# Recurrent stage of a two-layer encoder: units in cycles of two tiles, weights rounded by a second load, no products on GpSimd

## The chip, the cores and the metric

One core of one Trainium2 chip. The metric is the device time of one execution in microseconds (us): the median of three executions. One more execution was profiled, and every row below comes from that one.

## What is computed

An encoder trunk of two layers over 512 tokens of width 1024, in float32. Layer 0 mixes tokens with a bidirectional gated linear recurrence, layer 1 with dilated window attention; a convolutional feed-forward block follows each. The change lies in the recurrent mixer alone:

```
gate, u = split(x @ w_in, 2)                       # 1024 -> 2 x 1280
u = depthwise_conv(u, conv_w, conv_b)              # width 4
# per direction d (forward, backward), per block of 80 channels
r = sigmoid(ub @ w_a[d] + b_a[d]);  i = sigmoid(ub @ w_x[d] + b_x[d])
log_a = -8 * softplus(-lam[d]) * r;  a = exp(log_a)
h_d = scan(h <- a*h + sqrt(-expm1(2*log_a)) * (i*u))   # backward: from the end
y = gelu(gate) * (h_fwd + h_bwd);  out = y @ w_out  # 1280 -> 1024
```

After it come `layer_norm(alpha*x + out)` and the feed-forward block.

## The kernel before

**Tiles.** The 1280 channels of the recurrence are ten tiles of 128 channels by 512 tokens. A matrix product is made of float32 operands that are each split into two parts of the matmul's format fp32r, `hi` (rounded) and `lo` (the rest), and three passes: hi·hi, hi·lo, lo·hi (`passes`, L203). A weight piece of 128x1024 takes three steps: a DMA into `wraw`, a rounding into `whi` (L149 on VectorE for odd pieces, L151 on ScalarE for the others), and the subtraction into `wlo` on VectorE (L152). `weights(i)` keeps pieces loaded six units ahead and split three ahead (`RGA`).

**Units.** TensorE works through thirty units, each 24 matmuls of 512 columns: `u` (ten units, the convolution's input), `g` (gates: four banks r, i, r, i of six matmuls, forward then backward) and `y` (the GeLU branch, banks named `gb`). `SEQ` sets their order; u0 and u1 are made ahead in halves by `first_units`. After them comes the product with `w_out` (`token_phase`: ten pieces; five of them over all tokens, then five more token tile by token tile, `RTAIL`).

**Work of one tile.** `conv(t)`: ScalarE scales the bank (L445), VectorE adds three taps (L448), ScalarE makes `hi` (L337), VectorE `lo` (L338). A gate unit reads the tile's own pair and the neighbour's channels; for tiles 1, 2, 3, 6, 7, 8 these are put together into `side` by two VectorE copies (L467, L468). `g_unit(t)`: sigmoids (L493) and tanh (L496) on ScalarE, then i·u on GpSimd (L501). `decay` takes groups of 2, 3, 3 and 2 tiles (`SUBS`): exp (L517) on ScalarE, its square on GpSimd (L519; on VectorE, L523, for the last two tiles), weight (L524) on VectorE, root (L529) on ScalarE, then for each tile i·u times the weight (L533), two scans (L535, L536) on VectorE and their sum on GpSimd (L537). The GeLU branch is copied out of its bank (L561), turned by GeLU (L567) late and multiplied (L577), then split (L580, L585).

**What sets the order.** Every engine runs its instructions in the order in which the program issues them, and waits at the head of its queue. In the stage this order is that of the loops, with `decay`'s steps put off by hand-written counts of ticks (`DL`, `SP`, `SPE`, `PSP`; a tick is three matmuls). Loads stand on SP's queue; a gate piece is first cleared by GpSimd (L192) and then filled by 6 to 10 small DMAs (L196). Buffers of 4 KB per partition come from an arena of 40 slots, and 8 PSUM banks from another.

Of the kernel before, what the change touches and what calls it, by code (L numbers as in the profile page):

```python
# [56 lines left out]
def encoder(ctx: ExitStack, tc: tile.TileContext, x, ln_g, ln_b, rg_w_in, rg_conv_w, rg_conv_b,  # L57
# [73 lines left out]
    raws, parts, dead = {}, {}, set()  # L131
    at = {"load": 0, "split": 0}

    def load_to(i):
        while at["load"] <= min(i, len(loaders) - 1):
            j = at["load"]
            raws[j] = sb.get([128, 1024], F32, "wraw")
            loaders[j](raws[j])
            at["load"] += 1

    def split_to(i, pool=False):
        while at["split"] <= min(i, len(loaders) - 1):
# [3 lines left out]
            hi = sb.get([128, 1024], F32R, "whi")  # L146
# [5 lines left out]
            (nc.gpsimd if pool else nc.vector).tensor_tensor(lo, raw, f(hi), OP.subtract)  # L152
            sb.put(raw)
# [54 lines left out]

    queues = []
# [80 lines left out]
    def token_phase(i0, lhs, nk, free_lhs, last=False, tail=TAIL):  # L290
# [3 lines left out]
        def mm(t, h, k):  # L294
            if k == 0:
# [3 lines left out]
                   [v[:, 512 * h:512 * h + 512] for v in w], k == 0, k == nk - 1)  # L299

# [88 lines left out]
    SUBS = (1, 4, 7, 9)  # L389
    SEQ = "u0 u1 u2 g0 u3 u4 u5 g1 u6 y0 g2 u7 g3 g4 u8 g5 u9 g6 y1 g7 y2 g8 y3 g9 y4 y5 y6 y7 y8 y9"  # L390
    SEQ = [(u[0], int(u[1])) for u in SEQ.split()]
    DL = (4, 6, 3, 4, 1)
    SP = 4
    SPE = 2
    PSP = 1
# [3 lines left out]
    def add_rglru():  # L399
        for kind, t in SEQ:  # L400
            if kind == "g":
                add_gates(t)
            else:
                add_cols(rg_w_in[0], (DR if kind == "u" else 0) + 128 * t)
# [3 lines left out]
    def rglru(i0, raw, load_next):  # L408
# [70 lines left out]
        def g_unit(t):  # L479
            sd, own = side(t)  # L480
# [5 lines left out]
            for m in range(4):  # L486
# [6 lines left out]
                nc.scalar.activation(dst[:, d], b, AF.Sigmoid, bias=tab[:, bias + d * NR + t:bias + d * NR + t + 1])  # L493
                ps.put(b)
                if m % 2 == 0:
                    nc.scalar.activation(th[t][:, d], r[t][:, d], AF.Tanh, scale=p8[:, d * NR + t:d * NR + t + 1])  # L496
            done(i)
            if own:
                sb.put(sd)
            u = u32[t][:, t % 2]  # L500
            nc.gpsimd.tensor_tensor(ii[t], ii[t], u[:, None, :].to_broadcast([128, 2, 512]), OP.mult)  # L501
            if t % 2:
                sb.put(u32[t])
# [5 lines left out]
        def decay(sub):  # L509
            e2 = {}  # L510
            n = len(sub)
            end = sub[-1] == NR - 1
            for t in sub:
                e2[t] = sb.get([128, 2, 512], F32, "e2")
                for d in range(2):
# [605 lines left out]
```

## Time and profile before

| | us |
|---|---|
| median of 3 executions | 1602.05 |
| lowest, highest | 1598.27, 1602.62 |
| the profiled execution | 1604.17 |
| its span in the trace | 1602.40 |
| TensorE busy, share of the span | 1554.2, 97% |
| VectorE, ScalarE, GpSimd busy | 957.6, 646.5, 198.9 |
| mean granted TensorE clock | 0.992 |

A busy engine in such a page is one that had an instruction under way. TensorE's mean says little about one stage: the recurrent stage is the first 217 us, and has to be read in stretches of its own. Brackets behind a row of a timeline give the idle time of that engine just before the row, and what ended it.

### The profile page before, as it was taken

How to read it: one execution, taken by the hardware profiler on the slowest of the kernel's cores; microseconds unless marked ns; L12 is line 12 of the kernel's file. 1: busy time of each engine (PE TensorE's matmuls, PEld its weight loads, DVE VectorE, ACT ScalarE, POOL GpSimd, SP SyncE). 2: the span in 40 equal slices, each digit the busy share in tenths (PEclk: the TensorE clock that was granted, in tenths of full speed). 3: DMA queues.
4: the chain of work that ended last, by engine and by line, in shares of the span. 5: the costliest groups of instructions: out<-in, count | busy, mean ns of one | idle time of the engine just before them, and what ended most of it. 6: DMA issues, size and time to landing. Idle time of an engine off the chain costs nothing.

```text
span 1602.4 us, 20933 instructions
## 1 busy us (share of the span) xinstructions
PE 1554.2 (97%) x8115; PEld 1317.3 (82%) x8115; DVE 957.6 (60%) x1323; ACT 646.5 (40%) x1051; POOL 198.9 (12%) x379
## 2 busy tenths in 40 slices
PE   7987889999999999999999999999999999999998
PEld 6866668988888888989889988988988888888886
DVE  5689985554444324567567578567667444445225
ACT  3567651333333321355365355455452333334210
POOL 2254411100000001103001001201202000000001
PEclk9999999999999999999999999999999999999999
DMA  4222273222223331324343524333524322223311
GB/s 139 70 53 69 74 234 92 80 80 79 80 78 108 128 118 48 98 80 150 100 119 102 148 80 128 124 104 94 169 86 146 88 79 79 79 79 111 134 71 53
DMA packets 211151, 161.49 MB, mean 101 GB/s; under 512 B 16846, under 2 KB 189164, under 8 KB 211052
## 3 DMA queue, kind: packets, MB, share of 16 engines
q1 hardware_dynamic: 209900, 155.96, 32.0%
q0 software_dynamic: 1152, 4.19, 0.8%
q8 instruction: 64, 1.05, 0.3%
q14 instruction: 35, 0.29, 0.1%
HBM read 137.05 MB, written 2.10 MB: 87 GB/s over the span
## 4 chain that ended last, share of the span: by engine, by line
PE 82%; DVE 8%; ACT 3%; issue 3%; POOL 2%; DMA 1%; SPq 1%; DVEq 0%; ACTq 0%; POOLq 0%
PE v L205 22%; PE o L205 20%; PE g L205 15%; PE qk L205 15%; DVE wlo L152 2%; PE tP L878 2%; PE oT L906 1%; PE oT L903 1%; DVE th L536 1%; PE s L773 1%; PE u L205 1%; PE s L772 1%; PE q L205 1%; DVE th L533 1%; PE k L205 1%
## 5 line engine op out<-in xcount | busy, mean ns | idle before, releaser
L152 DVE TENSOR_TENSOR wlo<-wraw,whi 128x1024 fp32r<-128x1024 f32 x247 | 314.4, 1283 | 200.4 <-ACT whi L151 167.5
L151 ACT ACTIVATE whi<-wraw 128x1024 fp32r<-128x1024 f32 x237 | 246.2, 1052 | 115.8 <-PE o L205 105.7
L205 PE MATMUL o<-whi,h 128*128 128x512 f32 x704 | 217.3, 389 | 0.0
L205 PEld LDWEIGHTS o<-whi,h 128*128 128x128 f32 x704 | 132.1, 188 | 27.5
L205 PE MATMUL qk<-xhi,whi 128*128 128x512 f32 x352 | 146.1, 415 | 0.0
L205 PE MATMUL g<-xlo,whi 128*128 128x512 f32 (+1 forms) x384 | 144.6, 376 | 1.5 <-DVE xlo L280 1.5
L205 PE MATMUL g<-xhi,whi 128*128 128x512 f32 (+1 forms) x384 | 144.5, 376 | 0.3 <-ACT xhi L279 0.2
L205 PE MATMUL v<-xhi,whi 128*128 128x512 f32 (+1 forms) x384 | 144.5, 376 | 0.0
L205 PE MATMUL v<-xhi,wlo 128*128 128x512 f32 (+1 forms) x384 | 144.3, 376 | 0.0
L205 PE MATMUL g<-xhi,wlo 128*128 128x512 f32 (+1 forms) x384 | 144.3, 376 | 0.0
L205 PE MATMUL v<-xlo,whi 128*128 128x512 f32 (+1 forms) x384 | 144.3, 376 | 0.0
L205 PE MATMUL qk<-xhi,wlo 128*128 128x512 f32 x352 | 139.4, 396 | 0.0
L205 PE MATMUL qk<-xlo,whi 128*128 128x512 f32 x352 | 139.0, 395 | 0.0
L205 PE MATMUL o<-wlo,h 128*128 128x512 f32 x352 | 136.9, 389 | 0.0
L349 DVE SCALAR_TENSOR_TENSOR t<-g,fft,t 128x511 f32<-128x511 f32 x44 | 33.0, 750 | 116.7 <-ACT t L347 116.6
L205 PE MATMUL v<-whi,xhi 128*128 128x256 f32 x352 | 100.8, 286 | 0.0
L205 PE MATMUL v<-whi,xlo 128*128 128x256 f32 x352 | 99.2, 282 | 0.0
L205 PE MATMUL v<-wlo,xhi 128*128 128x256 f32 x352 | 99.1, 281 | 0.0
L803 ACT ACTIVATE P<-P,stats 128x256 f32<-128x256 f32 x128 | 63.6, 498 | 80.8 <-DVE stats L801 80.7
L347 ACT ACTIVATE t<-g,fft 128x512 f32<-128x512 f32 x44 | 34.2, 778 | 138.0 <-PE g L205 138.0
L205 PEld LDWEIGHTS g<-xlo,whi 128*128 128x128 f32 x384 | 72.2, 188 | 16.2 <-DVE xlo L280 1.9
L205 PEld LDWEIGHTS g<-xhi,whi 128*128 128x128 f32 x384 | 72.2, 188 | 14.9 <-ACT xhi L279 0.8
(205 smaller groups left out, 3150.5 us busy)
## 6 DMA issues: line engine op xcount, KB each, us to landing
wraw<-in_ff_w_up_dram SPq DMA_DIRECT2D x88, 512.0 KB, 3.7
wraw<-in_at_w_qkv_dram SPq DMA_DIRECT2D x72, 512.0 KB, 4.3
wraw<-in_ff_w_down_dram SPq DMA_DIRECT2D x44, 512.0 KB, 3.2
wraw<-in_rg_w_in_dram SPq DMA_DIRECT2D x20, 512.0 KB, 4.7
V<-vst SPq DMA_DIRECT2D x128, 64.0 KB, 2.1
k<-k SPq DMA_DIRECT2D x48, 128.0 KB, 2.2
kl<-kl SPq DMA_DIRECT2D x48, 128.0 KB, 2.2
wraw<-in_rg_w_out_dram SPq DMA_DIRECT2D x10, 512.0 KB, 3.3
```

Of the source, the lines that this page charges most:

```text
L151: nc.scalar.activation(hi, raw, AF.Copy)
L152: (nc.gpsimd if pool else nc.vector).tensor_tensor(lo, raw, f(hi), OP.subtract)
L205: nc.tensor.matmul(o, lhs[a], rhs[b], start=start and n == 0, stop=stop and n == 2, skip_group_check=skip)
L347: nc.scalar.activation(t1, bg, AF.Identity, bias=tab[:, 3 * NF + fi:3 * NF + fi + 1], scale=tab[:, NF + fi:NF + fi + 1])
L349: nc.vector.scalar_tensor_tensor(t1[:, 1:], bg[:, :511], tab[:, fi:fi + 1], t1[:, 1:], op0=OP.mult, op1=OP.add)
L533: nc.vector.tensor_tensor(h, h, ii[t], OP.mult)
L536: nc.vector.tensor_tensor_scan(h[:, 1, ::-1], r[t][:, 1, ::-1], h[:, 1, ::-1], 0.0, OP.mult, OP.add)
L772: nc.tensor.matmul(b[:, c], qa[:, h, c], ka[:, h, c], start=True, stop=False)
L773: nc.tensor.matmul(b[:, c], qa[:, h, c], kl[:, h, c], start=False, stop=True)
L803: nc.scalar.activation(P[:, b, :], P[:, b, :], AF.Exp, bias=st[:, w, 0, h, b:b + 1], scale=0.125, accum_out=st[:, w, 1, h, b:b + 1])
L878: nc.tensor.transpose(tb[:, 128 * n:128 * n + 128], a, ident)
L903: nc.tensor.matmul(ov0, v(0, s), pt[:, n, 0:256].rearrange("p (b r i) -> p r b i", b=2, r=4), start=(s == 0 and n == 0), stop=False, skip_ ...
```

## The change

1. **Order of units.** `SEQ` becomes cycles of two tiles: two `u`, two `g`, two `y`. The input units run one cycle ahead.
2. **Rounded weights.** For `u` and `y` pieces from the seventh on (16 pieces) a second DMA, issued by GpSimd, loads the same 512 KB of DRAM into the fp32r tile `whi` (`rounded`); the rounding on VectorE or ScalarE goes. Other pieces are all rounded by ScalarE.
3. **No products on GpSimd.** i·u and the sum of the two scans go to VectorE, the square of the exponential goes to ScalarE. GpSimd keeps clearing gate pieces, the small preparation of the decay rates, and the new loads.
4. **Neighbours' channels** (`side`) are put together by two SP DMAs in place of two VectorE copies.
5. **GeLU** is read straight from the bank, for two tiles at a time; the decay chain runs for pairs.
6. **Pieces.** The side work is cut into single pieces with a rank, a cost and what they depend on. `pump`, called at every tick, issues a piece on VectorE or ScalarE when that engine is booked less than 1.4 us ahead of the tick's planned time. `need` issues what a gate unit or the output product reads.

```diff
 def load_to(i):
             raws[j] = sb.get([128, 1024], F32, "wraw")
             loaders[j](raws[j])
+            if j in rounded:
+                his[j] = sb.get([128, 1024], F32R, "whi")
+                rounded[j](his[j])
 def split_to(i, pool=False):
+            hi = his.pop(j, None)
+            if hi is None:
+                hi = sb.get([128, 1024], F32R, "whi")
+                nc.scalar.activation(hi, raw, AF.Copy)
+                book("s", 1.05)
-            if j % 2 and j < 3 * NR:
-                nc.vector.tensor_copy(hi, raw)
-            else:
-                nc.scalar.activation(hi, raw, AF.Copy)
+    def take(eng, limit):
+        for p in sorted(side_work[eng]):
+            rank, n, cost, makes, deps, fn = p
+            if all(d in due and due[d] <= limit for d in deps):
+                side_work[eng].remove(p)
+                due[makes] = book(eng, cost, deps)
+                fn()
+                return True
+        return False
+    def pump():
+        now = clock[0] * TICK
+        for eng in ("s", "v"):
+            while side_work[eng] and booked[eng] <= now + SLK and take(eng, now + SLK):
+                pass
-    SEQ = "u0 u1 u2 g0 u3 u4 u5 g1 u6 y0 g2 u7 g3 g4 u8 g5 u9 g6 y1 g7 y2 g8 y3 g9 y4 y5 y6 y7 y8 y9"
+    SEQ = "u0 u1 u2 u3 g0 g1 y0 y1 u4 u5 g2 g3 y2 y3 u6 u7 g4 g5 y4 y5 u8 u9 g6 g7 y6 y7 g8 g9 y8 y9"
 def make_side(t):
-                nc.vector.tensor_copy(v[0:64], f(uhl[t + 1][0:64]))
-                nc.vector.tensor_copy(v[64:128], f(uhl[t - 1][64:128]))
+                nc.sync.dma_start(f(v[0:64]), f(uhl[t + 1][0:64]))
+                nc.sync.dma_start(f(v[64:128]), f(uhl[t - 1][64:128]))
 def g_unit(t):
+            need(("ul", max(t - 1, 0)), ("ul", t), ("ul", min(t + 1, NR - 1)))
-            nc.gpsimd.tensor_tensor(ii[t], ii[t], u[:, None, :].to_broadcast([128, 2, 512]), OP.mult)
+            def gated():
+                nc.vector.tensor_tensor(ii[t], ii[t], u32[t][:, t % 2][:, None, :].to_broadcast([128, 2, 512]), OP.mult)
 def decay(...)
-                    nc.gpsimd.tensor_tensor(e2[t], r[t], r[t], OP.mult)
+                nc.scalar.activation(e2[t], r[t], AF.Square)
-                nc.gpsimd.tensor_tensor(h[:, 0], h[:, 0], h[:, 1], OP.add)
+            def both(t):
+                nc.vector.tensor_tensor(th[t][:, 0], th[t][:, 0], th[t][:, 1], OP.add)
+            piece("s", 1, 4.1, ("a", pr), (("g", pr[-1]),), exps)
+            for t in pr:
+                piece("s", 1, 1.05, ("q", t), (("a", pr),), lambda t=t: square(t))
+                piece("v", 1, 1.22, ("w", t), (("q", t),), lambda t=t: weight(t))
+            piece("s", 1, 3.4, ("s", pr), tuple(("w", t) for t in pr), root)
 def y_unit(t):
-            nc.scalar.activation(ga[t][:, t % 2], b, AF.Gelu_apprx_tanh if direct else AF.Copy)
+                def gelu():
+                    for n in pr:
+                        nc.scalar.activation(ga[:, n % 2], yb[n], AF.Gelu_apprx_tanh)
+                        ps.put(yb.pop(n))
```

**Where it moves instructions.** VectorE at the start of the stage, before: behind the rates' `RECIPROCAL` stand tile 0 (taps, `lo`), tile 1 and then weights.

```order
L425 RECIPROCAL sp_s2_285<-sp_s2_285 128x20
L448 SCALAR_TENSOR_TENSOR u32_320<-u_137,rgt_281,u32_320 128x510
L448 SCALAR_TENSOR_TENSOR u32_320<-u_137,rgt_281,u32_320 128x511 x2
L338 TENSOR_TENSOR u_325<-u32_320,u_325 128x512
L448 SCALAR_TENSOR_TENSOR u32_320<-u_138,rgt_281,u32_320 128x510
L448 SCALAR_TENSOR_TENSOR u32_320<-u_138,rgt_281,u32_320 128x511 x2
L338 TENSOR_TENSOR u_332<-u32_320,u_332 128x512
```

The same place after the change; `wlo_394` belongs to y0's piece, the first that GpSimd loads, and L507 is the `lo` of tiles 0 and 1.

```order
L469 RECIPROCAL sp_s2_295<-sp_s2_295 128x20
L156 TENSOR_TENSOR wlo_340<-wraw_141,whi_338 128x1024
L156 TENSOR_TENSOR wlo_344<-wraw_191,whi_342 128x1024
L498 SCALAR_TENSOR_TENSOR u32_330<-u_131,rgt_291,u32_330 128x510
L498 SCALAR_TENSOR_TENSOR u32_330<-u_131,rgt_291,u32_330 128x511 x2
L498 SCALAR_TENSOR_TENSOR u32_330<-u_132,rgt_291,u32_330 128x510
L498 SCALAR_TENSOR_TENSOR u32_330<-u_132,rgt_291,u32_330 128x511 x2
L156 TENSOR_TENSOR wlo_394<-wraw_346,whi_348 128x1024
L507 TENSOR_TENSOR u_381<-u32_330,u_381 128x512
L507 TENSOR_TENSOR u_403<-u32_330,u_403 128x512
```

Three weights now stand ahead of the `lo` of tile 0, and the third reads a tile that GpSimd's DMA fills. GpSimd at that place, before: the last step of the rates (L436), the clearing of g1's piece, then products and clearings.

```order
L436 TENSOR_SCALAR sp_n8_286<-sp_p8_287 128x20
L192 MEMSET wraw_352 128x1024
L501 TENSOR_TENSOR i_408<-i_408,u32_320 128x1024
L192 MEMSET wraw_450 128x1024
L192 MEMSET wraw_541 128x1024
L192 MEMSET wraw_588 128x1024
L501 TENSOR_TENSOR i_597<-i_597,u32_320 128x1024
```

And after; the first clearing is that of g2's piece.

```order
L480 TENSOR_SCALAR sp_n8_296<-sp_p8_297 128x20
L176 DMA whi_348<-in_rg_w_in_dram 128x8x128
L176 DMA whi_352<-in_rg_w_in_dram 128x8x128
L176 DMA whi_356<-in_rg_w_in_dram 128x8x128
L176 DMA whi_398<-in_rg_w_in_dram 128x8x128
L202 MEMSET wraw_436 128x1024
L202 MEMSET wraw_499 128x1024
```

Four loads stand between the rates and g2's clearing. SP's queue after the change, at the end of g2's copies: `side_458` is tile 1's, `side_490` tile 2's.

```order
L206 DMA wraw_436<-in_rg_w_a_dram 16x2x64
L206 DMA wraw_436<-in_rg_w_x_dram 16x2x64
L527 DMA side_458<-u_432 64x1024
L528 DMA side_458<-u_381 64x1024
L527 DMA side_490<-u_481 64x1024
L528 DMA side_490<-u_403 64x1024
```

The neighbours' copies are new on this queue, and tile 1's stands behind g2's eight copies, which wait for the clearing.

## Rows read from the trace of the kernel before

**Rows 1.** Stretches: span, busy us (x instructions) by engine, clock, DMA share, GB/s.
```profile
26.19:217.01 190.82, 165.37 (x676) 128.56 (x674) 166.96 (x151) 116.97 (x159) 83.96 (x64) 0.96 0.25 70
40.39:51.59 11.20, 11.20 (x50) 9.01 (x49) 7.36 (x8) 7.40 (x10) 3.29 (x2) 1.00 0.43 110
57.18:62.64 5.46, 5.46 (x26) 4.50 (x24) 4.57 (x7) 1.30 (x2) 0.00 (x0) 1.00 0.50 125
141.80:146.97 5.17, 5.17 (x12) 4.08 (x13) 4.39 (x5) 5.10 (x8) 0.00 (x0) 0.51 0.40 99
```
**Rows 2.** Timeline of TensorE: start, us, instruction [idle before, what ended it].
```profile
141.80 1.19 PE L205 MATMUL gate<-u,whi 128*128 128x512 f32 x2 [6.95 <-DVE u L448]
217.01 0.49 PE L205 MATMUL o<-whi,y 128*128 128x512 f32 x1 [1.12 <-ACT whi L151]
```
**Rows 3.** Groups of TensorE, 26 to 240 us: busy us, mean ns | idle before.
```profile
L205 PE MATMUL gate<-u,whi 128*128 128x512 f32 x112 | 36.7, 408 | 14.3 <-DVE u L448 10.0 <-ACT u L337 2.2 <-ACT r L493 1.4
L205 PE MATMUL gate<-u,wlo 128*128 128x512 f32 x56 | 22.6, 404 | 1.3 <-DVE wlo L152 1.3
```
**Rows 4.** Groups of VectorE, 26.19 to 217.01 us.
```profile
L152 DVE TENSOR_TENSOR wlo<-wraw,whi 128x1024 fp32r<-128x1024 f32 x27 | 47.4, 1760 | 3.6 <-ACT whi L151 2.6
L524 DVE SCALAR_TENSOR_TENSOR th<-e,th 128x1024 f32<-128x1024 f32 x10 | 17.1, 1724 | 7.1 <-POOL e L519 7.1
L535 DVE TENSOR_TENSOR_SCAN th<-r,th 128x512 f32<-128x512 f32 x10 | 16.2, 1624 | 0.3
L448 DVE SCALAR_TENSOR_TENSOR u<-u,rgt,u 128x511 f32<-128x511 f32 x20 | 15.0, 750 | 0.7
```
**Rows 5.** Groups of GpSimd and ScalarE, the same stretch.
```profile
L501 POOL TENSOR_TENSOR i<-i,u 128x1024 f32<-128x1024 f32 x10 | 28.7, 2871 | 51.0 <-ACT i L493 41.1 <-issue 9.9
L151 ACT ACTIVATE whi<-wraw 128x1024 fp32r<-128x1024 f32 x14 | 14.7, 1049 | 0.0
L517 ACT ACTIVATE r<-r,sp_n 128x512 f32<-128x512 f32 x20 | 12.7, 711 | 0.0
L529 ACT ACTIVATE th<-th 128x1024 f32<-128x1024 f32 x10 | 10.2, 1054 | 10.9 <-DVE th L524 10.8
L517 ACT ACT_TABLE_LOAD x4 | 5.1, 1283 | 0.1
```
**Rows 6.** Timelines of VectorE, then of GpSimd.
```profile
34.94 0.69 DVE L338 TENSOR_TENSOR u<-u,u 128x512 fp32r<-128x512 f32 x1 [0.76 <-ACT u L337]
104.87 1.23 DVE L152 TENSOR_TENSOR wlo<-wraw,whi 128x1024 fp32r<-128x1024 f32 x1
110.16 3.47 DVE L152 TENSOR_TENSOR wlo<-wraw,whi 128x1024 fp32r<-128x1024 f32 x1
...
110.15 2.40 POOL L501 TENSOR_TENSOR i<-i,u 128x1024 f32<-128x1024 f32 x1 [0.89 <-ACT i L493]
```
**Rows 7.** Timeline of GpSimd: first and last step of the rates, what follows.
```profile
28.08 0.23 POOL L426 TENSOR_TENSOR sp_q<-sp_q,sp_s 128x20 f32<-128x20 f32 x1 [26.10 <-ACT u L445]
37.94 1.18 POOL L436 TENSOR_SCALAR sp_n<-sp_p 128x20 f32<-128x20 f32 x1
39.06 0.95 POOL L192 MEMSET wraw<- 128x1024 f32 x1
```
**Rows 8.** DMAs of 512 KB issued by GpSimd: ns of issue, us to landing.
```profile
L246 POOL DMA_DIRECT2D lng<-in_ln_g_dram x4: 595/599/777, 207.5 to 1464.1; - x4
...
DMA to landing us min/median/max: 4.3/4.5/5.2
```
**Rows 9.** DMAs issued by SP: KB each, median us to landing; one gate copy.
```profile
wraw<-in_rg_w_in_dram SPq DMA_DIRECT2D x20, 512.0 KB, 4.7
wraw<-in_rg_w_out_dram SPq DMA_DIRECT2D x10, 512.0 KB, 3.3
k<-k SPq DMA_DIRECT2D x48, 128.0 KB, 2.2
...
41.35 0.43 SPq L196 DMA_DIRECT2D wraw<-in_rg_w_x_dram  x1
```

More of the change, by code (lines that the diff above doesn't have):

```diff
@@ L206, in passes, with book, piece, need @@
                              skip_group_check=skip)
+    TICK, SLK = 0.69, 1.4
+    booked = {"v": 0.0, "s": 0.0}
+    due = {}
+    side_work = {"v": [], "s": []}
+    def book(eng, cost, deps=()):
+        start = max([booked[eng], clock[0] * TICK] + [due[d] for d in deps])
+        booked[eng] = start + cost
+        return booked[eng]
+    def piece(eng, rank, cost, makes, deps, fn):
+        heapq.heappush(side_work[eng], (rank, next(order), cost, makes, deps, fn))
+    def take(eng, limit):
[12 more added lines that the diff above has]
+                pass
+    def need(*keys):
+        for key in keys:
+            while key not in due:
+                assert take("s", 1e9) | take("v", 1e9), key
     queues = []
@@ L403, in add_rglru @@
             else:
-                add_cols(rg_w_in[0], (DR if kind == "u" else 0) + 128 * t)
+                add_cols(rg_w_in[0], (DR if kind == "u" else 0) + 128 * t, len(loaders) >= 6)
         for k in range(NR):
@@ L521, in weight, with inputs @@
             def weight(t):
-                if end:
-                    nc.vector.tensor_tensor(e2[t], r[t], r[t], OP.mult)
                 nc.vector.scalar_tensor_tensor(th[t], e2[t], 1.0, th[t], op0=OP.add, op1=OP.mult)
-                sb.put(e2[t])
+                sb.put(e2.pop(t))
             def root():
-                for t in sub:
+                for t in pr:
                     nc.scalar.activation(th[t], th[t], AF.Sqrt)
-            def scan(t):
+            def inputs(t):
+                nc.vector.tensor_tensor(th[t], th[t], ii[t], OP.mult)
+                sb.put(ii.pop(t))
@@ L538, in scan @@
-                sb.put(r[t])
-            now = clock[0] + (DL[0] if end else DL[1])
-            for m, t in enumerate(sub):
-                at_tick(now + DL[2] * m, lambda t=t: weight(t))
-            now += DL[2] * (n - 1) + DL[3]
-            at_tick(now, root)
-            for m, t in enumerate(sub):
-                at_tick(now + DL[4] + (SPE if end else SP) * m, lambda t=t: scan(t))
-            if end:
-                at_tick(now + 1, gelu)
-                for m in range(sub[0]):
-                    at_tick(now + DL[4] + SPE * n + PSP * m, ready)
@@ L570, in ready @@
[L570 to L587 removed]
+                sb.put(r.pop(t))
@@ new lines, in rglru @@
+        yb = {}
+        def y_unit(t):
+            yb[t] = bank("gb")
+            cols_unit(yb[t], next(it))
+            if t % 2:
+                pr = (t - 1, t)
+                ga = sb.get([128, 2, 512], F32, "ga")
+                left[pr] = 2
+                def gelu():
+                    for n in pr:
+                        nc.scalar.activation(ga[:, n % 2], yb[n], AF.Gelu_apprx_tanh)
+                        ps.put(yb.pop(n))
+                piece("s", 1, 2.7, ("ga", pr), (), gelu)
+                for n in pr:
+                    product(n, pr, ga[:, n % 2], ga)
@@ new lines, in product, with times, high, low @@
+        def product(t, pr, g, ga):
+            def times():
+                nc.vector.tensor_tensor(g, g, th[t][:, 0], OP.mult)
+                sb.put(th.pop(t))
+            def high():
+                y[t] = pair("y")
+                nc.scalar.activation(y[t][:, 0], g, AF.Copy)
+            def low():
+                nc.vector.tensor_tensor(y[t][:, 1], g, f(y[t][:, 0]), OP.subtract)
+                left[pr] -= 1
+                if not left[pr]:
+                    sb.put(ga)
+            piece("v", 3, 0.69, ("p", t), (("ga", pr), ("h", t)), times)
+            piece("s", 3, 0.63, ("yh", t), (("p", t),), high)
+            piece("v", 3, 0.69, ("yl", t), (("yh", t),), low)
```

142 lines of the change are left out of this document (64 added, 78 removed).

## Prediction

> **What bounds the kernel now.** I read the busy times by stretch first. TensorE is busy nearly all the span, so the change can win only what TensorE loses in the recurrent stage. That stage is read from unit u2, at 26.19 us, to the first matmul of the output product, at 217.01 us: 190.82 us, of which TensorE is busy 165.37 [rows 1]. Twenty-eight units lie in it. Two `u` units back to back take 11.20 us, so a `u` or `y` unit takes 5.60, and a gate unit takes 5.46 at full clock [rows 1]. Unhindered, the 18 units of the first kind and ten gate units need 18 x 5.60 + 10 x 5.46 = 155.4 us. **The stage loses 35.4 us**: 25.4 idle, and 10.0 at a lower clock, as after the longest wait (6.95 us [rows 2]), when two gate banks took 5.17 us at a granted clock of 0.51, the level of 1.2 GHz [rows 1]; at full clock two banks of four are half of 5.46, so that cost 2.4 us.
>
> Next, who is waited for. The longest waits end with VectorE (taps, weights) [rows 2, 3], which is busy 167 of the 191 us [rows 1]. Its groups show why: the subtraction into `wlo` takes 1.23 us alone and 3.47 beside GpSimd's product of i and u [rows 6]; its mean is 1.76, that of the weight 1.72, that of the scan 1.62 [rows 4]. Against 1.23, these three groups lose 27 x 0.53 + 10 x 0.49 + 10 x 0.39 = 23 us. GpSimd's i·u, for its part, takes 2.87 us [rows 5]. So VectorE sets the stage's pace, and GpSimd sets VectorE's.
>
> **The change, part by part.**
>
> *Products off GpSimd.* VectorE gets ten i·u of 1.23 us and ten sums of half that width, 0.69 as the `lo` of the same width [rows 6]: +19.2 us. It loses some 13 roundings (0.69 us where nothing stretches them, the time of a `lo`) and 12 neighbour copies of as much: -17.3 us. The squares it also loses are 2 x 1.23 us. So the count is even, and the stretching of at least 23 us goes: 167 - 23 = 144 us at most, over units that need 155. ScalarE gets ten squares, as long as a root of 1.05 us [rows 5], and about seven table loads of 1.28 us, since each of five cycles goes through sigmoid, exp, root and GeLU; it loses some ten half-width steps of the GeLU branch, under 0.71 us each: 117 + 10.5 + 9.0 - 6 = 130 us of work. Both then lie under TensorE's 155.4, and **TensorE becomes the bound**. What remains is waits.
>
> *Start of the stage.* This is a new wait. VectorE's queue has `wlo_394` ahead of the `lo` of tiles 0 and 1, and it reads a tile that GpSimd loads. GpSimd issues that load only after the rates, which ran from 28.08 to 39.06 us [rows 7]. Some of those small steps were stretched by VectorE (the last took 1.18 us, the first 0.23); now two `wlo` fall on earlier steps, so I take 38.2. Queued behind it on VectorE: both `lo`, and all of tile 2 and 3; who waits is g0. A load issued by GpSimd lands 4.5 us after issue [rows 8]; it was of 4 KB rows. With SP, 512-byte rows (`rg_w_in`) land 4.7 us after issue and 4 KB rows (`rg_w_out`) 3.3: +1.4 [rows 9]. Unknown is the issue: 0.60 us for 128 rows, and now 1,024 pieces. Its bounds are 0.6, if the count is nothing, and eight times the 0.60 to 0.78 of the rows, 4.8 to 6.2; I take 1.2, nearer to the row that is the same instruction with the same bytes, which adds 0.6. So it lands at 38.2 + 4.5 + 1.4 + 0.6 = 44.7; `wlo` 1.23 and `lo` 0.69 make 46.6. TensorE has ended u3 at 26.2 + 11.2 = 37.4: **9.2 us lost**, plus 2.4 for the clock as after the 6.95 us wait. Before, the wait there was 2.2 [rows 3], part of the 35.4.
>
> The Trainium skill (DMA: Bandwidth & Descriptors, Anatomy of one DMA) fits a load by GpSimd as 2.0 us plus its bytes over 436 GB/s, 3.2 us here. By it the sum would be 1.3 us lower. The row of 4.5 us speaks against it, and I keep the row.
>
> *Neighbours by DMA.* Tiles 1, 3 and 7 are read soon after they are made. After the first landing VectorE does the two `lo` (to 47.3), three taps of 0.75, a `wlo` and a `lo`: 51.5. A copy is half of 512 KB: between 2.2 us (128 KB) and 3.3 (512 KB) [rows 9], with its issue landed by 54.3 to 55.5. g1 asks at 46.6 + 5.46 + 2.4 + 0.7 = 55.2. For g3 and g7 the cover is a unit u, a unit g and one half bank, 11.8 us, over taps, `hi`, `lo`, a scan or two ahead in the queue and the copy, some 10. I put 1.0 us for the three, with 0 and 6 as ends.
>
> *Other loads by GpSimd.* They are issued six units ahead and split three ahead: three units, 16.8 us, cover about 6.5. Cost nothing; without the cover each load's landing would stand in VectorE's queue. DMA engines were 25% busy [rows 1], and 16 loads of 512 KB in some 160 us add 52 GB/s to 70.
>
> *Small waits.* Gate banks waited 1.4 us for ScalarE and 1.3 for `wlo` [rows 3]: I keep 3 us.
>
> *The end.* The last pair's chain and the ten `w_out` pieces now stand beside the output product, which reads the last five tiles only after five pieces over all tokens. From the end of g9 that is two y units and five pieces, 7 x 5.60 = 39.2 us. VectorE has in it two weights, two i·u, two inputs, four scans and ten `wlo` (20 x 1.23), two sums and some eight products and `lo` (10 x 0.69): 31.5 us; ScalarE has four exps, two squares, two roots, ten `whi`, three tables, and GeLUs and `hi` of some eight half widths: 2.8 + 2.1 + 2.1 + 10.5 + 3.8 + 5.7 = 27 us. Both fit, but one waits for the other in turn (exps, weights, roots, scans, products); walked through in the order of the two queues, the last `wlo` ends only about a microsecond before TensorE asks. I count no loss, with 0 and 4 us as ends.
>
> **Sum.** Losses after: 9.2 + 2.4 + 1.0 + 3.0 = 15.6 us; before: 35.4. The output product starts 19.8 us earlier, at 197.2. The rest of the program is the same code. The profiled execution took 1604.17 us (a span of 1602.40 and 1.77 around it), so the sum is 1584.4 for it; it was 2.12 above the median, and against the median of 1602.05 the forecast is **1582**.
>
> **Rivals.**
>
> *Dear issue (1598).* If an issue takes 5.5 us, the middle of the far bound, the first load lands at 49.0 and g0 starts its second pass at 50.9: 13.5 + 2.4. GpSimd's queue then has four issues, to 60.2, before it clears g2's piece; SP's has g2's eight copies of 0.43 behind that, and tile 1's neighbours behind those: 61.2 + 3.5 + 3.3 = 68, where g1 asks at 59.5. That is 8.5 + 2.4 more: 31 us lost, 1598. For it: GpSimd makes the pieces one by one in no row shown; against it: nothing shows the issue growing. Up to 2 us each it stays near the forecast.
>
> *Issue over 6.4 us: slower.* The same chain with an issue P: the neighbours land at 38.2 + 4P + 1 + 3.5 + 3.3, and 26 units and the clock follow, so the output product starts near 191.4 + 4P. At P = 6.4 that is 217, no change; at 8 us 223.4, **1608**. The trap is that side data stand behind loads that are in no hurry. The far bound, 6.2, ends just below. The Trainium skill (SBUF — State Buffer, the box on "DVE blocks DMA" under SBUF: two separate sides) says such issues starve, 0.62 us becoming 3.1, beside VectorE copies that use both ports; by it each of the first four issues would cost 2.5 us more. No row here shows that, and the change takes the copies and roundings from VectorE in this stage; 0.78 us is the slowest issue [rows 8].
>
> *Queues in step (1594).* The order is fixed by planned costs, and a piece that is late holds everything behind it. From the last sigmoid of a pair ScalarE has three tables, four exps, two squares, two `whi`, two roots and two GeLUs (0.71 each at most): 3.8 + 2.8 + 2.1 + 2.1 + 2.1 + 1.4 = 14.4 us before the next `u` can be scaled, under 2 y and 1 u, 16.8. If waits for VectorE in between take 5 us, four cycles lose 2.6 to 3 each: 12 us.
>
> *Does not pay (1602).* All of these at once, VectorE's queue staying the bound through waits in its head in place of stretching.
>
> **How the numbers follow.** Forecast 0.57 (1571 to 1590), queues in step 0.15, dear issue 0.10, no gain 0.10, slower 0.08. The low end: a start that loses 7 us with its clock (the rates over at 37, the load landing in the 4.5 of the row) and nothing else, 28.4 us won, and 2.5 of the output product's own waits and clock: 1571. The high end is the dear issue, 1598. About 0.3%, 4.8 us, is what a measurement of this kernel can tell from no change. Faster by more: forecast, queues in step and half the dear issue's 0.10 (cheaper than 5.5 us), 0.77; within: the other half and no gain, 0.15; slower: 0.08.
>
> **What would show it.** VectorE's `wlo`, weights and scans at 1.2 us throughout; a TensorE wait near 37 us ended by a `lo` at about 46 to 47, followed by a few us at half clock; GpSimd's loads at about 1 us of issue; hardly a wait above 2 us afterwards; the output product's first matmul near 197. Wrong would be: issues of 4 us or more, a second long wait in g1 ended by a DMA, waits of 3 us in every cycle ended by ScalarE, or waits within the output product for y8 and y9.

## The result, and the profile after

The changed kernel took 1577.82 us (median of four executions, 1574.23 to 1578.61), the kernel before 1600.91 beside it: a ratio of 0.9853, 95% interval 0.9831 to 0.9874, some 23 us less. The profiled executions differ by 25.6 us (1578.61 against 1604.17; spans 1576.8 and 1602.40). The stretches of the changed kernel that answer to [rows 1] are the recurrent stage and the output product up to its transposes (columns: span, busy us by engine TensorE, weight load, VectorE, ScalarE, GpSimd, granted clock, DMA share, GB/s).

```profile
26.18:195.20 169.02, 159.32 (x676) 128.31 (x674) 124.17 (x139) 126.88 (x165) 30.77 (x52) 0.97 0.65 160
195.20:250.50 55.30, 55.30 (x249) 45.82 (x248) 43.31 (x53) 19.11 (x23) 4.53 (x3) 1.00 0.42 126
```

The output product of the kernel before, cut in the same way:

```profile
217.01:275.06 58.05, 57.29 (x248) 47.10 (x249) 37.74 (x48) 16.51 (x21) 5.06 (x4) 0.97 0.46 147
```

**Where the time went.** The stage is 21.80 us shorter, the output product 2.75, and the remaining 1.05 lies in the unchanged rest. Against the 155.4 us that the units need, the stage loses 13.6 us where it lost 35.4: 169.02 - 159.32 = 9.7 idle and 3.9 at half clock. The idle part is three waits; these are all of them (timeline of TensorE; in brackets the idle time before the row and what ended it). The waits of [rows 2, 3] that ended with taps, `wlo` and sigmoids are gone. The 3.9 us at half clock are the rest of the 13.6; 3.5 of them are read off behind the first two waits (1.9 and 1.7, see the section on the prediction).

```profile
44.41 0.80 PE L215 MATMUL gate<-u,whi 128*128 128x512 f32 x1 [6.55 <-DVE u L507]
...
54.34 0.90 PE L215 MATMUL gate<-side,whi 128*128 128x512 f32 x2 [2.17 <-DMA side<-u]
...
90.46 0.70 PE L215 MATMUL gate<-side,whi 128*128 128x512 f32 x2 [0.97 <-DMA side<-u]
```

The groups of VectorE and GpSimd, 26 to 210 us, answer to [rows 4, 5] (busy us, mean ns of one, idle time before): each VectorE operation is back at the 1.2 us that it takes undisturbed, and the product of i and u is one of them.

```profile
L156 DVE TENSOR_TENSOR wlo<-wraw,whi 128x1024 fp32r<-128x1024 f32 x32 | 38.9, 1220 | 34.1 <-ACT whi L153 25.1 <-DMA whi<-in_rg_w_in_dram 7.2 <-PE gate L215 1.8
L570 DVE TENSOR_TENSOR i<-i,u 128x1024 f32<-128x1024 f32 x10 | 12.2, 1220 | 5.0 <-ACT i L554 4.9
L593 DVE SCALAR_TENSOR_TENSOR th<-e,th 128x1024 f32<-128x1024 f32 x10 | 12.0, 1220 | 4.4 <-ACT e L590 4.4
L610 DVE TENSOR_TENSOR_SCAN th<-r,th 128x512 f32<-128x512 f32 x9 | 10.9, 1207 | 0.0
...
L176 POOL DMA_DIRECT2D whi<-in_rg_w_in_dram x16 | 14.4, 907 | 60.8 <-DVE wlo L156 16.0 <-PE u L215 14.7 <-DVE th L601 11.7
```

The start of the stage, which the prediction worked out step by step: GpSimd's last step of the rates and its first four loads, VectorE's `wlo` that reads the first of them with both `lo` behind it, and SP's second copy for tile 1's neighbours.

```profile
37.75 0.26 POOL L480 TENSOR_SCALAR sp_n<-sp_p 128x20 f32<-128x20 f32 x1
37.95 3.80 POOL L176 DMA_DIRECT2D whi<-in_rg_w_in_dram  x4
...
42.53 1.23 DVE L156 TENSOR_TENSOR wlo<-wraw,whi 128x1024 fp32r<-128x1024 f32 x1 [7.16 <-DMA whi<-in_rg_w_in_dram]
43.67 1.29 DVE L507 TENSOR_TENSOR u<-u,u 128x512 fp32r<-128x512 f32 x2
...
49.53 0.60 SPq L528 DMA_DIRECT2D side<-u  x1
```

### The profile page after: what moved, and what is told of

It reads as the page before. It is cut to its first block, busy times and chain, and to the rows that moved or that the text cites. A ratio compares the mean times of both kernels' runs of the same rounds, so it can differ in the third digit from the quotient of the medians.

```text
span 1576.8 us, 20972 instructions
## 1 busy us (share of the span) xinstructions
PE 1545.2 (98%) x8115; PEld 1316.6 (83%) x8115; DVE 920.5 (58%) x1314; ACT 662.4 (42%) x1062; POOL 145.8 (9%) x367
## 3 DMA queue, kind: packets, MB, share of 16 engines
q8 instruction: 64, 1.05, 0.3%
## 4 chain that ended last, share of the span: by engine, by line
PE 89%; DVE 4%; issue 2%; POOL 1%; DMA 1%; ACT 1%; SPq 1%; DVEq 0%; POOLq 0%; ACTq 0%
PE v L215 23%; PE o L215 20%; PE g L215 16%; PE qk L215 15%; PE gb L215 3%; PE gate L215 2%; PE u L215 2%; PE tP L943 2%; PE oT L971 1%; PE oT L968 1%; PE s L838 1%; PE s L837 1%; PE q L215 1%; PE k L215 1%; PE tx L323 1%
## 5 line engine op out<-in xcount | busy, mean ns | idle before, releaser
L156 DVE TENSOR_TENSOR wlo<-wraw,whi 128x1024 fp32r<-128x1024 f32 x247 | 300.1, 1225 | 225.3 <-ACT whi L153 187.6
```

## Experiments: what made the gain

The theory behind the prediction: products on GpSimd stretched VectorE, VectorE's busy time set the pace, and without them TensorE becomes the bound. The rival: what set the pace was the order in which work stands in the queues, so that the cycles of units, or the pacing, made the gain. Four kernels take one part away from the changed kernel or give it alone to the kernel before (a_pool, a_unpaced, b_nopool, b_seq); four follow up what those showed (b_late, a_oldseq, a_slack4, a_ballast); the last four of the table take the start apart (next section). All medians stand beside executions of the kernel before on the same chip; the chips differ from kernel to kernel, so a difference in microseconds between two changed kernels is good to a few of them, and the ratio is the sounder number.

| kernel | median, us | against before (95%) |
|---|---|---|
| changed kernel | 1577.82 | 0.9853 (0.9831 to 0.9874) |
| a_pool: products back on GpSimd | 1585.88 | 0.9893 (0.9876 to 0.9909) |
| a_unpaced: pacing off | 1610.43 | 1.0049 (1.0032 to 1.0067) |
| a_slack4: slack four times as large | 1583.62 | 0.9891 (0.9876 to 0.9905) |
| a_oldseq: old order of units | 1580.98 | 0.9867 (0.9849 to 0.9885) |
| a_ballast: idle products on GpSimd | 1593.71 | 0.9950 (0.9934 to 0.9967) |
| b_nopool: before, products moved | 1609.81 | 1.0047 (1.0032 to 1.0062) |
| b_late: the same, i·u issued later | 1598.35 | 0.9976 (0.9967 to 0.9986) |
| b_seq: before, new order of units | 1604.37 | 1.0016 (1.0006 to 1.0025) |
| a_soft10: loads by GpSimd from piece 10 | 1575.46 | 0.9830 (0.9816 to 0.9845) |
| a_nosoft: no loads by GpSimd | 1580.61 | 0.9870 (0.9838 to 0.9902) |
| a_sidevec: neighbours by VectorE | 1580.11 | 0.9866 (0.9836 to 0.9896) |
| a_both: a_soft10, tile 1's neighbours by VectorE | 1568.29 | 0.9791 (0.9763 to 0.9819) |

**b_nopool**, the kernel before with the products moved and nothing else.

```diff
-            nc.gpsimd.tensor_tensor(ii[t], ii[t], u[:, None, :].to_broadcast([128, 2, 512]), OP.mult)
+            nc.vector.tensor_tensor(ii[t], ii[t], u[:, None, :].to_broadcast([128, 2, 512]), OP.mult)
...
-                    nc.gpsimd.tensor_tensor(e2[t], r[t], r[t], OP.mult)
+                    nc.scalar.activation(e2[t], r[t], AF.Square)
...
-                nc.gpsimd.tensor_tensor(h[:, 0], h[:, 0], h[:, 1], OP.add)
+                nc.vector.tensor_tensor(h[:, 0], h[:, 0], h[:, 1], OP.add)
```

> The kernel before with only the products moved: i·u and sum to VectorE, square to ScalarE; old order of units, old loads and copies. Theory A: the stretch of some 33 us goes, 19 us of work come, VectorE 167 + 19 - 33 = 153 us, and the stage gets 8 to 20 us shorter: 1582 to 1594. Rival B: the old order keeps its waits, less than 4 us either way: 1598 to 1606.

Measured: 1609.81, slower than before by 0.3 to 0.6%. Neither theory had that. The stretching is gone, as theory A says, and VectorE's busy time fell from 167 to 152 us, but the stage grew from 190.82 to 198.45 us. The group of `wlo`, 26 to 215 us, and the stage (columns as above):

```profile
L152 DVE TENSOR_TENSOR wlo<-wraw,whi 128x1024 fp32r<-128x1024 f32 x25 | 30.5, 1224 | 6.5 <-ACT whi L151 5.4 <-DMA wraw<-in_rg_w_in_dram 0.3
...
26.19:224.64 198.45, 170.48 (x672) 132.64 (x670) 151.77 (x170) 125.38 (x167) 18.43 (x36) 0.91 0.24 68
```

VectorE's longest wait (us in total, times, longest):

```profile
DVE i L501 <- ACT i L493: 21.4, 5, 7.4
```

VectorE's timeline ahead of one TensorE wait, and that wait:

```profile
89.61 0.69 DVE L149 CAST whi<-wraw 128x1024 fp32r<-128x1024 f32 x1
90.41 1.22 DVE L152 TENSOR_TENSOR wlo<-wraw,whi 128x1024 fp32r<-128x1024 f32 x1
91.55 1.22 DVE L533 TENSOR_TENSOR th<-th,i 128x1024 f32<-128x1024 f32 x1
92.80 1.23 DVE L535 TENSOR_TENSOR_SCAN th<-r,th 128x512 f32<-128x512 f32 x1
93.94 1.20 DVE L536 TENSOR_TENSOR_SCAN th<-r,th 128x512 f32<-128x512 f32 x1
95.18 0.69 DVE L537 TENSOR_TENSOR th<-th 128x512 f32<-128x512 f32 x1
95.79 1.22 DVE L501 TENSOR_TENSOR i<-i,u 128x1024 f32<-128x1024 f32 x1
96.92 1.22 DVE L152 TENSOR_TENSOR wlo<-wraw,whi 128x1024 fp32r<-128x1024 f32 x1
98.06 2.31 DVE L448 SCALAR_TENSOR_TENSOR u<-u,rgt,u 128x510 f32<-128x510 f32 x3
...
100.52 1.19 PE L205 MATMUL gate<-u,whi 128*128 128x512 f32 x2 [4.89 <-DVE u L448]
```

Every operation here runs at its undisturbed length. The taps at 98.06 are what TensorE waits for, and they stand behind 8.5 us of work that TensorE does not wait for here, 4.3 of them after ScalarE had scaled the tile (at 93.8). In the kernel before, this wait ended at 100.90, so up to here nothing was won or lost. What was lost came after: VectorE stood 21.4 us in all with a product at the head of its queue, waiting for ScalarE's sigmoids; it was GpSimd that used to wait for them, 41.1 us ahead of its products [rows 5]. One of these waits, the rounding behind it, and TensorE waiting for that rounding:

```profile
133.77 1.23 DVE L501 TENSOR_TENSOR i<-i,u 128x1024 f32<-128x1024 f32 x1 [6.23 <-ACT i L493]
134.91 0.69 DVE L149 CAST whi<-wraw 128x1024 fp32r<-128x1024 f32 x1
...
135.74 1.19 PE L205 MATMUL gate<-u,whi 128*128 128x512 f32 x2 [3.65 <-DVE whi L149]
```

**So VectorE's busy time was not what set the pace: what stands ahead in its queue was.** The Trainium skill (TensorE: Matmul & The Clock Gate, table at its head) gives VectorE, ScalarE and GpSimd strictly first-in first-out queues; these rows of VectorE agree.

**b_late**: the same kernel, i·u issued just ahead of the tile's weight.

```diff
             def weight(t):
+                u = u32[t][:, t % 2]
+                nc.vector.tensor_tensor(ii[t], ii[t], u[:, None, :].to_broadcast([128, 2, 512]), OP.mult)
+                if t % 2:
+                    sb.put(u32[t])
```

> The kernel before with the products moved off GpSimd, as in b_nopool, and the VectorE product i·u issued not right behind its gate unit but just ahead of the tile's weight, some ticks later. In b_nopool VectorE stood 21.4 us at the head of its queue in front of these ten products, waiting for ScalarE's sigmoids. If that place in the queue is what ate the gain: idle time ahead of i·u under 5 us, TensorE's waits shrink, and the time is 1585 to 1600 us, under the kernel before. Rival (the old order of units has other waits of the same length behind these): 1604 to 1612 us, as b_nopool.

Measured: 1598.35, 11.5 us under b_nopool, with the same instructions on the same engines. The wait ahead of the product is gone (group of VectorE):

```profile
L519 DVE TENSOR_TENSOR i<-i,u 128x1024 f32<-128x1024 f32 x10 | 12.2, 1219 | 0.0
```

The place in the queue decided, but with all the products moved and i·u better placed the old code gains only 0.24%, not the 8 to 20 us of theory A: its TensorE still waits for taps, 6.17 us at 141.2, where [rows 2] had 6.95.

**b_seq**, the new order of units alone (with the decay in five pairs).

```diff
-    SUBS = (1, 4, 7, 9)
-    SEQ = "u0 u1 u2 g0 u3 u4 u5 g1 u6 y0 g2 u7 g3 g4 u8 g5 u9 g6 y1 g7 y2 g8 y3 g9 y4 y5 y6 y7 y8 y9"
+    SUBS = (1, 3, 5, 7, 9)
+    SEQ = "u0 u1 u2 u3 g0 g1 y0 y1 u4 u5 g2 g3 y2 y3 u6 u7 g4 g5 y4 y5 u8 u9 g6 g7 y6 y7 g8 g9 y8 y9"
```

> The kernel before with only the new order of units, and decay by pairs (five groups in place of four); products on GpSimd, old loads, old copies, hand-written ticks. Theory A: VectorE stays stretched and late: within 6 us of 1601, or slower. Rival B: the order alone gives most of it: 1580 to 1590.

Measured: 1604.37, no gain. The old code turns the whole GeLU branch only after the last roots, so the longest wait is now one at the output product (the hand-written ticks were left as they were for the old order):

```profile
217.00 0.80 PE L205 MATMUL o<-whi,y 128*128 128x512 f32 x1 [16.47 <-ACT y L580]
```

**a_oldseq**, the opposite: all of the change but the order.

```diff
-    SEQ = "u0 u1 u2 u3 g0 g1 y0 y1 u4 u5 g2 g3 y2 y3 u6 u7 g4 g5 y4 y5 u8 u9 g6 g7 y6 y7 g8 g9 y8 y9"
+    SEQ = "u0 u1 u2 g0 u3 u4 u5 g1 u6 y0 g2 u7 g3 g4 u8 g5 u9 g6 y1 g7 y2 g8 y3 g9 y4 y5 y6 y7 y8 y9"
-    RGA = [6, 3]
+    RGA = [5, 3]
```

> The changed kernel with the old order of units (y units late, g units close after their u), and pieces loaded five units ahead in place of six, since the old order keeps more buffers alive; pacing, products on VectorE and ScalarE, second loads and DMA copies as changed. If pacing with the products moved is what gains, whatever the order: within 5 us of 1578. Rival (the paced pieces need the cycles, which put two y units of cover between a pair's gates and what reads them): gate units wait for taps and neighbours at each g close behind its u, the GeLU branch piles up at the end, 1588 us or more.

Measured: 1580.98; its interval overlaps that of the changed kernel. The old order, under which the kernel before waited 25.4 us in the stage, now has three TensorE waits above 1 us before the output product (1.75 at g0 and the first two rows) and one in it:

```profile
35.73 0.79 PE L215 MATMUL gate<-u,whi 128*128 128x512 f32 x1 [1.60 <-DVE u L507]
...
142.43 0.69 PE L215 MATMUL gate<-side,whi 128*128 128x512 f32 x2 [2.88 <-DMA side<-u]
...
196.12 0.73 PE L215 MATMUL o<-whi,y 128*128 128x512 f32 x2 [1.94 <-DVE y L656]
```

**The order of units is thus not what gained.** What it gives is room: with pieces loaded six units ahead, the old order needs more than the arena's 40 buffers, hence the five here.

**a_unpaced**: a piece is issued as soon as what it depends on has been issued.

```diff
-    TICK, SLK = 0.69, 1.4
+    TICK, SLK = 0.69, 1e9
```

> The changed kernel with the pacing switched off: a piece is issued as soon as what it depends on has been issued, however far the engine is booked ahead (the slack of 1.4 us becomes boundless). If single paced pieces carry the gain: queues hold urgent taps and lo behind long chains, gate units wait 2 us or more in most cycles, 1588 us or more. Rival: the order and the lighter VectorE carry it, within 4 us of 1578.

Measured: 1610.43, 32.6 us more than the changed kernel, with the same instructions on the same engines. VectorE's waits for sigmoids ahead of its products, as in b_nopool, are longer (4.9 us in the changed kernel), and so are the waits of its decay weights for the squares (4.4 there), here in us in total, times, longest:

```profile
DVE i L570 <- ACT i L554: 16.3, 6, 3.5
...
DVE th L593 <- ACT e L590: 13.3, 4, 3.6
```

TensorE's waits are as long as before the change. Ahead of the one at 172.85, VectorE worked off the decay chain of a pair, weights and the GeLU products from 147.83 on, before it came to the taps of a tile that this gate unit needs (164.50); SP's second neighbours' copy could follow only at 168.84:

```profile
54.08 1.19 PE L215 MATMUL gate<-side,whi 128*128 128x512 f32 x2 [10.81 <-DMA side<-u]
...
164.50 2.31 DVE L498 SCALAR_TENSOR_TENSOR u<-u,rgt,u 128x510 f32<-128x510 f32 x3
...
168.84 0.60 SPq L528 DMA_DIRECT2D side<-u  x1
...
172.85 1.22 PE L215 MATMUL gate<-side,whi 128*128 128x512 f32 x2 [7.13 <-DMA side<-u]
...
206.23 0.79 PE L215 MATMUL gb<-xhi,whi 128*128 128x512 f32 x1 [4.64 <-ACT r L554]
...
228.07 0.79 PE L215 MATMUL o<-whi,y 128*128 128x512 f32 x1 [4.44 <-ACT ga L639]
```

**a_slack4** puts the slack at 5.6 us, one TensorE unit (`SLK = 5.6`).

> The changed kernel with a slack of 5.6 us in place of 1.4 (a TensorE unit ahead in place of a quarter). If what hurts is work standing far ahead in a queue, a unit's worth costs some of the 32 us that boundless slack costs: 1582 to 1595 us. Rival (only the whole chain of a pair put in at once hurts): within 3 us of 1578.

Measured: 1583.62, 5.8 us more. Even a unit's worth of work ahead shows. The wait of 2.17 us at g1 is now:

```profile
54.73 1.19 PE L215 MATMUL gate<-side,whi 128*128 128x512 f32 x2 [10.74 <-DMA side<-u]
```

There is no wait of 6.55 us ahead of it: g0 goes earlier here, and g1 takes the loss, which makes the two together 2.0 us longer. The larger part is a new wait of 3.10 us for neighbours at 159.79. The output product starts at 199.52, 4.3 us later than in the changed kernel.

**a_pool** puts the three products of the changed kernel back on GpSimd, at the places of the pieces.

```diff
-                nc.vector.tensor_tensor(ii[t], ii[t], u32[t][:, t % 2][:, None, :].to_broadcast([128, 2, 512]), OP.mult)
+                nc.gpsimd.tensor_tensor(ii[t], ii[t], u32[t][:, t % 2][:, None, :].to_broadcast([128, 2, 512]), OP.mult)
...
-                nc.scalar.activation(e2[t], r[t], AF.Square)
+                nc.gpsimd.tensor_tensor(e2[t], r[t], r[t], OP.mult)
...
-                nc.vector.tensor_tensor(th[t][:, 0], th[t][:, 0], th[t][:, 1], OP.add)
+                nc.gpsimd.tensor_tensor(th[t][:, 0], th[t][:, 0], th[t][:, 1], OP.add)
```

> The changed kernel with its three kinds of product back on GpSimd (i·u, square, sum of scans), everything else as changed. Theory A (products on GpSimd stretch VectorE, and that set the pace): VectorE's wlo, weights and scans show means of 1.5 us or more again in place of 1.22, pieces run late, and at least half of the gain of some 24 us goes: 1590 to 1602 us. Rival B (order and pacing made the gain, the place of the products hardly matters): VectorE's busy time is then about 124 - 19 + 30 = 135 us, still well under TensorE's 155, so within 4 us of 1578.

Measured: 1585.88, 8 us more, between the two. The stretching is all back (compare 1760 in [rows 4]), and a gate unit waits where none did. Even so the output product starts only 1.6 us later (196.78). Most of the loss, 5.3 us, comes after that, with three waits of 0.69 to 1.49 us in the output product and lower clock behind them. The group of `wlo`, 26 to 215 us:

```profile
L156 DVE TENSOR_TENSOR wlo<-wraw,whi 128x1024 fp32r<-128x1024 f32 x31 | 53.8, 1742 | 24.0 <-ACT whi L153 16.4 <-DMA whi<-in_rg_w_in_dram 7.0 <-DMA wraw<-in_rg_w_in_dram 0.6
```

TensorE's timeline:

```profile
158.59 0.73 PE L215 MATMUL gate<-side,whi 128*128 128x512 f32 x2 [3.03 <-DMA side<-u]
```

**a_ballast** leaves the changed kernel as it is and adds products on GpSimd that nobody reads, 30 of them.

```diff
+        idb = ident[:, None, :].to_broadcast([128, 8, 128])
+        def ballast(n):
+            scr = sb.get([128, 8, 128], F32, "scr")
+            nc.gpsimd.tensor_tensor(scr[:, :n], idb[:, :n], idb[:, :n], OP.mult)
+            sb.put(scr)
```

> The changed kernel plus products on GpSimd that nobody reads (one of 128x1024 beside each i·u and each square, one of 128x512 beside each sum; input is the identity, output a buffer that is given back), so that the contention comes without a chain through GpSimd. If contention alone costs: VectorE's wlo mean 1.4 us or more in place of 1.22 and 3 to 9 us more, 1581 to 1587 us; of the 8 us that the products on GpSimd cost, most is then stretching. Rival (it is the longer chain through GpSimd): within 2.5 us of 1578.

Measured: 1593.71, 15.9 us more: dearer than real products. Since they wait for no data, GpSimd runs them in a row as soon as it is free, at the worst place (rows of VectorE, GpSimd and TensorE; the first product begins 1.2 us after the `wlo` that it stretches):

```profile
42.59 4.50 DVE L156 TENSOR_TENSOR wlo<-wraw,whi 128x1024 fp32r<-128x1024 f32 x1 [7.00 <-DMA whi<-in_rg_w_in_dram]
47.02 4.67 DVE L507 TENSOR_TENSOR u<-u,u 128x512 fp32r<-128x512 f32 x2
...
43.75 1.95 POOL L585 TENSOR_TENSOR scr<-ident 128x1024 f32<-128x1024 f32 x1
46.55 6.90 POOL L585 TENSOR_TENSOR scr<-ident 128x1024 f32<-128x1024 f32 x3
...
49.45 0.80 PE L215 MATMUL gate<-u,whi 128*128 128x512 f32 x1 [11.42 <-DVE u L507]
```

The `wlo` of 1.23 us took 4.50 and the two `lo` of 1.29 took 4.67, and g0 began 5 us later than in the changed kernel. So the contention is real without any chain through GpSimd, and its price hangs on which VectorE operation it meets. The loss is not contention alone: the buffers of the idle products are waited for once (2.1 us).

## Experiments: the start of the stage

**a_soft10**: the first four loads by GpSimd are replaced by ScalarE's rounding.

```diff
-                add_cols(rg_w_in[0], (DR if kind == "u" else 0) + 128 * t, len(loaders) >= 6)
+                add_cols(rg_w_in[0], (DR if kind == "u" else 0) + 128 * t, len(loaders) >= 10)
```

> The changed kernel with GpSimd's loads from piece 10 on in place of piece 6: the first four (y0, y1, u4, u5) are rounded by ScalarE, so the wlo ahead of the lo of tiles 0 and 1 waits for no load. If that load is what g0 waits for: the wait of 6.55 us at 37.9 us goes with 2 us of half clock behind it, 1569 to 1571 us. Rival: g0 then waits for something else that comes as late (taps, ScalarE's table and roundings, the gate pieces): 1575 to 1580.

Measured: 1575.46, 2.4 us less, where 7 to 9 were expected; the two intervals overlap, but in the trace the output product starts 4.2 us earlier (190.97). The wait of g0 is gone; that of g1 grew from 2.17 to 7.03 us (TensorE; SP's second copy for it):

```profile
50.48 1.19 PE L215 MATMUL gate<-side,whi 128*128 128x512 f32 x2 [7.03 <-DMA side<-u]
...
45.61 0.59 SPq L528 DMA_DIRECT2D side<-u  x1
```

SP issued the copies only behind g2's pieces, 1.8 us after the `lo` that they read was there (43.23), and g1 could go on 4.87 us after the second issue began: the copies themselves are the larger part. One wait hid the other.

**a_nosoft**: no loads by GpSimd at all (`False` for the condition above).

> The changed kernel without any load by GpSimd: all pieces are rounded by ScalarE, 16 x 1.05 = 16.8 us more there, 127 + 17 = 144 of some 160 us. If the second load is needed: ScalarE runs late, gate banks wait for it in each cycle, and the time is 1578 or more in spite of the start. If it isn't: the start's wait goes as without the first four loads, and the time is 1569 to 1573 us.

Measured: 1580.61; by time it can't be told from the changed kernel, but against a_soft10 it is 5 us more, and in the traces the output product starts 6.1 us later (197.04 against 190.97). A later gate unit waits too. Ahead of its copies, VectorE's `lo` (at 152.00) stands behind a subtraction that had to wait 0.58 us for one of ScalarE's new roundings (149.77); how much of the 3.95 us comes from that is not shown:

```profile
157.39 1.19 PE L215 MATMUL gate<-side,whi 128*128 128x512 f32 x2 [3.95 <-DMA side<-u]
```

The later loads are worth something; the first four save nothing that the times show.

**a_sidevec**: the neighbours by VectorE copies.

```diff
-                nc.sync.dma_start(f(v[0:64]), f(uhl[t + 1][0:64]))
-                nc.sync.dma_start(f(v[64:128]), f(uhl[t - 1][64:128]))
+                nc.vector.tensor_copy(v[0:64], f(uhl[t + 1][0:64]))
+                nc.vector.tensor_copy(v[64:128], f(uhl[t - 1][64:128]))
```

> The changed kernel with the neighbours' channels put together by VectorE copies as before (12 x 0.69 = 8.3 us more there) in place of SP's DMAs. If the copies by DMA only cost the wait of g1 (2.17 us and about 1.5 us of half clock): 1574 to 1576 us. Rival, VectorE has no room for them: waits of gate units for VectorE in later cycles, 1580 us or more.

Measured: 1580.11, not told from the changed kernel by time. The trace shows a gain that was lost again: g0 still waits (6.46 us), but no gate unit waits for neighbours, the output product starts at 190.82 instead of 195.20, and then it waits for the GeLU of the last pair:

```profile
198.67 0.79 PE L215 MATMUL o<-whi,y 128*128 128x512 f32 x1 [3.55 <-ACT ga L639]
```

**a_both**: loads by GpSimd from piece 10 on, and VectorE copies for tile 1 alone.

```diff
             if 0 < t % 5 < 4:
                 sides[t] = v = pair("side")
+                if t == 1:
+                    nc.vector.tensor_copy(v[0:64], f(uhl[t + 1][0:64]))
+                    nc.vector.tensor_copy(v[64:128], f(uhl[t - 1][64:128]))
+                    return
```

> The changed kernel with GpSimd's loads from piece 10 on and tile 1's neighbours put together by VectorE (the other five by DMA). If the two waits at the start are two separate losses, both go: the output product begins near 183 to 185 us in place of 195.2, and the time is 1565 to 1568 us. Rival: what is won at the start comes back as waits of later cycles, since VectorE and ScalarE have less lead: 1572 to 1578.

Measured: 1568.29, the fastest of all; its interval against the kernel before lies wholly below that of the changed kernel. The stage takes 157.47 us, 2.1 more than its units need (a stretch, as above):

```profile
26.40:183.87 157.47, 155.62 (x672) 125.81 (x672) 125.47 (x141) 129.64 (x169) 28.77 (x48) 1.00 0.63 156
```

g1's wait is 1.23 us (timeline of TensorE):

```profile
44.94 0.73 PE L215 MATMUL gate<-side,whi 128*128 128x512 f32 x2 [1.23 <-DVE side L529]
```

Nothing came back later: both waits at the start were losses of their own.

## Why the prediction was right, and where it was not

**The size: right.** 19.8 us were forecast for the profiled execution, 25.6 came. Losses in the stage: 15.6 forecast, 13.6 measured. The other 3.8 us are what the forecast left at zero: 2.75 in the output product, which before ran at a clock of 0.97 with a wait of 0.76 us inside it, and 1.05 in the rest. The 2.0 us between 15.6 and 13.6 are for the most part a balance: the start was put 3.2 us too dear with its clock and the small waits 3.0, the neighbours 3.8 too cheap.

**Products off GpSimd: right in the count, wrong as the cause.** VectorE was to be busy 144 us at most and ScalarE 130; they are busy 124 and 127, no operation is stretched, and TensorE is the bound. But the step "VectorE sets the stage's pace, and GpSimd sets VectorE's" doesn't hold. The products alone make the old code slower (b_nopool), and the changed kernel with stretched operations keeps nearly three quarters of its gain (a_pool). The term of 23 us was a sum of busy time put in place of waits, and from "VectorE and ScalarE lie under TensorE's 155" the prediction went on to nearly no waits. That doesn't follow: in b_nopool VectorE is busy 152 us of its stage and in a_unpaced 127, and TensorE stands idle some 28 us of it in both. The forecast came right because the pacing supplied what the argument lacked; to that extent the number is luck. The prediction knew the order in the queues only as a risk, "queues in step" and "does not pay": without the pacing the same instructions cost 1610 us (a_unpaced). How much pacing would gain under the old instructions and copies was not tried, nor was the GeLU read straight from the bank taken out by itself; of the parts given alone to the kernel before, the products lose, or gain 0.24% with i·u issued later, and the order gains nothing. ScalarE got four table loads more in the stage (19 against 15), where about seven were counted.

**The start: right in mechanism, 2.7 us too dear.** g0 was held by the `lo` behind `wlo_394`, as forecast: 6.55 us against 9.2. The rates ended at 38.0 (38.2 forecast). The load landed 4.6 us after its issue began, as the 4.5 of [rows 8]; the additions of 1.4 for short rows and 0.6 for the issue were most of the error. They were wrong for this load rather than for all: the 16 loads landed after 6.0 us at the median. The half clock behind it cost 1.9 us (26 matmuls from 44.41 to 52.17 at a granted clock of 0.78 on average, 7.76 us against 26/24 of 5.46), forecast 2.4. By the fit of the Trainium skill (DMA: Bandwidth & Descriptors, Anatomy of one DMA) the load would have taken 3.2 us, an estimate; the row of this kernel was the better guide.

**The issue: not dear.** The 16 issues took 0.88 to 1.14 us each, where 1.2 was taken between 0.6 and 6.2. With that both rivals on it fall. The chain that they feared cost g1 nothing here: g2's pieces were issued by 47.5 us, and the `lo` that tile 1's copies read was there only at 48.9. The starving that the Trainium skill (SBUF — State Buffer, box on "DVE blocks DMA" under SBUF: two separate sides) describes beside VectorE copies was not seen. The change had taken those copies out of the stage, and in a_sidevec and a_both, which put some back, none ran while GpSimd was issuing, so no run here shows it. The 0.62 and 3.1 us that the Trainium skill gives in the same section are for a whole DMA and not for its issue alone, as the prediction took them.

**Neighbours by DMA: too cheap.** 1.0 us was put, within 0 to 6; it was 2.17 + 0.97 idle and 1.7 at half clock behind the first (21 matmuls in 6.46 us at a granted clock of 0.74 on average, 4.78 at full clock). The copy's landing was the mis-sized term: 2.2 to 3.3 us were taken, 4.2 to 4.9 came. A long wait in g1 ended by a DMA was also among the prediction's signs of being wrong; here it is 2.17 us, and without the wait of g0 in front of it, it is 7.03 (a_soft10). Why the copies land so late stays open: the loads by GpSimd are not needed for it, since in a_nosoft, which has none, they took 3.8 and 4.1.

**Small waits and other loads.** 3 us were kept for waits on ScalarE and `wlo`; there is none. Only the first load was ever waited for.

**The end: right.** No wait inside the output product. The thin margin that the prediction named is there: a_sidevec, whose product starts 4.4 us earlier, waits 3.55 us for the GeLU. That a_both starts 11 us earlier and doesn't wait there shows that it hangs on how the pieces fall, not on the start alone.

## What to carry to other kernels

An engine with much busy time is not yet the bound: look at what stands ahead, in its queue, of the instruction that TensorE waits for, and whether that work was in a hurry. Moving work to an engine whose queue is then held by it (a product that waits for a sigmoid) can cost more than the stretching that it removes; issue side work piece by piece, close to when its inputs are there. When one wait at the start is removed, look which wait stood in its shadow before counting the gain.

## What the runs showed of the hardware

- Loads of 512 KB by GpSimd in 1,024 pieces of 512 bytes took 0.88 to 1.14 us to issue, against 0.60 to 0.78 for 128 rows [rows 8]: eight times the pieces, half as much again. They landed 4.1 to 8.1 us after issue, median 6.0.
- Two copies of 64x1024 from SBUF to SBUF by SP let the gate unit go on only 4.2 us (g3, second issue at 86.28) to 4.8 us (g1) after the second issue began; in the other runs with such a wait it was 3.8 (a_nosoft, a_pool) to 6.3 (a_soft10, at 86.21). Loads of 512 KB by SP had landed in 3.3 to 4.7 [rows 9].
- Beside products on GpSimd that it had nothing to do with, VectorE's `wlo` took 4.50 us in place of 1.23, and two `lo` 4.67 in place of 1.29 (a_ballast). In a_pool one `wlo` took 8.43 us (at 129.71), though it began 0.26 us before the first of three products beside it.
